# End of the attention: scaling passes for the projection's first weights and outputs on GpSimd, later splits behind the last turned keys

## The chip, the cores and the metric

One Trainium2 chip, one core. The metric is the device time of one execution in microseconds. Of the kernel before there are three timed runs: 2403.33, 2406.47 and 2407.38 us, median 2406.47. One more execution was profiled; every row of a profile here comes from it.

## What is computed

One inference step of a two-layer hybrid decoder in float32, for a prompt of 2048 tokens and 8 short samples of 4 tokens. Layer 0 runs a gated linear attention (4 heads) and a forgetting attention (4 heads of 128) side by side on one input projection; their gated outputs are put side by side and go through one output projection, whose result is added to the input. Layer 1 is a gated linear attention with its own projections. The place of this change is the end of the forgetting attention and the beginning of the output projection:

```python
logits = einsum('bthd,bshd->bhts', q, k) * scale + c_t - c_s      # causal, c = cumulative log forget values
p = softmax(logits);  o_b = einsum('bhts,bshd->bthd', p, v)
out = concatenate([o_a * silu(g_a), o_b * silu(g_b)]) @ w_out     # 1024 x 1024
x = x + out                                                        # then the next layer's RMSNorm
```

## The kernel before

A scheduler orders the instructions of each engine when the program is built; on the chip every engine takes its own queue strictly in that order, and waits where a value isn't there yet. SP's queue issues nearly all loads.

**Numbers as two halves.** TensorE multiplies float16. Every operand is split into `hi`, its float16 rounding, and `lo`, the float16 of what is left, and each product is three matmuls: hi·hi, hi·lo, lo·hi (`mm3`, lines 467 to 469). So weights and activations are scaled by a power of two and split before use. There are two ways to split a block of 128 x 512 values. In the short way ScalarE writes `hi` with the scale in it (L345 for weights, L1596 for outputs) and VectorE computes `lo` (L346, L1597). In the long way ScalarE first scales the raw block in place (L348, L1592), then writes `hi` from it unscaled (L349, L1593), and GpSimd subtracts to `lo` (L350, L1594). A weight unit of 1024 x 256 is four blocks, two of each way (`half_unit`); a piece of 256 tokens of the attention's outputs likewise (`y_pieces`, where `YPOOL` picks the blocks of the long way).

**The attention's end.** `fox_prompt` goes through 4 heads and 4 groups of 512 queries. For each block of 128 queries it computes scores `s`, adds the bias and takes the maximum on VectorE (L1200), the exponentials on ScalarE (L1208), sum and reciprocal on VectorE (L1211, L1212), and scales the rows on GpSimd (L1216). The rows `L` are then transposed on TensorE (L1236) into PSUM tiles `pt`. Such a transposed block is called a turned key here: ScalarE copies it to `th` (L1243), VectorE computes `tl` (L1244), and TensorE multiplies it with the values into `fo`. `fy` is `fo` times the gate (L1259) and goes to the outputs `yT` in memory by GpSimd's queue (L1261). The last group runs in two halves, the first with seven turned keys and the second with eight. Four buffers each hold `th` and `tl`.

**The output projection.** Four units of 256 columns (`out_units`). Unit 0 uses the raw buffer tag `yr` of two buffers, which the pieces of outputs use too: unit 0's raw weights and the first piece (`yr_19100`) take them first, the second piece (`yr_19222`) gets the weights' buffer, the third (`yr_19439`) the first piece's, and so on; the fifth piece (`yr_19463`) is the 32 sample tokens. `prepare`, mixed into the attention, splits unit 0's weights (`w_o_19102`) and the first two pieces. Behind the attention stand the other pieces, the loads of the nine row tiles of the input (L1826) and `dense(0, 3)`, which runs units 0 to 2 on TensorE and splits the next units' weights (`wr_o_19434` is unit 1's raw tile, `wr_o_19544` unit 2's, `wr_o_19613` unit 3's). The order in which the scheduler placed these among the attention's last instructions is not bound to anything but their data. A unit runs over four pairs of token tiles, then over the 32 sample rows (`few_rows`); each pair takes one of three PSUM buffers until VectorE has added it to its row tiles (L1642). SP's queue holds, in this order: unit 0's weights, pieces one and two, unit 1's weights, piece three, units 2 and 3, piece four, the next layer's first weights (`wr_Cv`), row tile 0, the sample piece, the other row tiles.

## Time and profile before

| | |
|---|---|
| median of three runs | 2406.47 us |
| the profiled execution | 2408.25 us |
| its span, first to last instruction | 2405.8 us |
| granted TensorE clock, mean of the span | 0.987 |
| busy: TensorE, VectorE, ScalarE, GpSimd | 2296.7, 1418.9, 1111.1, 744.1 us |
| first turned key of the last group's second half, on ScalarE | 1305.00 us |
| first matmul of the output projection | 1318.83 us |

Times inside the execution are microseconds from the start of the span. In a profile's row, PE is TensorE, PEld its weight loads, DVE VectorE, ACT ScalarE, POOL GpSimd, SPq the issuing queue of SP; `out<-in` names the tiles without buffer numbers, and L is the line of the kernel. A timeline row is start, duration, engine, line, operation, tiles, shape, count and, in brackets, the idle time ahead of it with what ended it. Rows of DMA issues end with the time to landing. A busy share is an average; what the change is worth is read from the stretch between about 1284 and 1345 us.

### The profile page before, as it was taken

To read this page: it belongs to the slowest core of one execution; us is meant where nothing else is said; L and a number is where in the kernel's file an instruction comes from. 1 tells how busy PE (TensorE), PEld (TensorE's weight loads), DVE (VectorE), ACT (ScalarE), POOL (GpSimd) and SP (SyncE) were. 2 spreads that over 40 slices of the span, in tenths; PEclk is the share of its full clock that TensorE was granted. 3 is DMA by queue.
4 is the path that set the end of the run, shared out by engine and by line. 5 is a ranking of instruction groups with operands and counts; after the bars stand their busy time and mean duration, and the time that the engine had idled before them with its cause. 6 is when DMAs were issued, how large, how long until landed. Compare 5 with 4: busy or idle time off the path is not lost. (4 is left out here: it accounts for less than half of the span.)

```text
span 2405.8 us, 58659 instructions
## 1 busy us (share of the span) xinstructions
PE 2296.7 (95%) x23324; PEld 1635.3 (68%) x23324; DVE 1418.9 (59%) x3345; ACT 1111.1 (46%) x2466; POOL 744.1 (31%) x839
## 2 busy tenths in 40 slices
PE   7999999999999999999997999999999999999998
PEld 5667668854655876655445876777678766666887
DVE  7556556546764548567667363665675644557554
ACT  6434243342433127466668254535443645545333
POOL 2233223112212225144465111432452222322222
PEclk9999999999999999999999999999999999999999
DMA  6231235435431276776865532122146312114453
GB/s 181 78 87 58 85 121 160 144 108 149 144 116 59 82 223 220 259 246 208 265 195 181 163 108 59 45 76 89 50 147 194 114 37 73 43 58 159 152 190 148
DMA packets 297013, 317.25 MB, mean 132 GB/s; under 512 B 39729, under 2 KB 241010, under 8 KB 296738
## 3 DMA queue, kind: packets, MB, share of 16 engines
q1 hardware_dynamic: 295234, 308.98, 40.7%
q8 instruction: 183, 3.00, 0.5%
q0 software_dynamic: 1504, 4.52, 0.5%
q14 instruction: 92, 0.75, 0.1%
HBM read 242.31 MB, written 71.11 MB: 130 GB/s over the span
## 5 line engine op out<-in xcount | busy, mean ns | idle before, releaser
L469 PE MATMUL pt_o<-w_o,act 128*128 128x256 f16 x1024 | 281.2, 275 | 4.1 <-DVE act L1597 3.9
L467 PE MATMUL pt_o<-w_o,act 128*128 128x256 f16 x1024 | 281.5, 275 | 2.4 <-ACT sg1C L523 2.4
L468 PE MATMUL pt_o<-w_o,act 128*128 128x256 f16 x1024 | 281.2, 275 | 0.0
L467 PEld LDWEIGHTS <-act 128*128 128x128 f16 x2304 | 226.9, 98 | 37.0 <-ACT act L462 4.7
L469 PEld LDWEIGHTS <-act 128*128 128x128 f16 x2304 | 226.8, 98 | 35.2 <-DVE act L1597 5.1
L468 PEld LDWEIGHTS <-act 128*128 128x128 f16 x2304 | 227.0, 99 | 33.6 <-issue 3.7
L467 PE MATMUL pt_Cv<-w_Cv,act 128*128 128x256 f16 (+1 forms) x512 | 140.3, 275 | 1.7 <-ACT act L462 0.9
L468 PE MATMUL pt_Cv<-w_Cv,act 128*128 128x256 f16 (+1 forms) x512 | 140.0, 274 | 0.0
L469 PE MATMUL pt_Cv<-w_Cv,act 128*128 128x256 f16 (+1 forms) x512 | 139.7, 274 | 0.0
L633 POOL TENSOR_TENSOR kA<-kA,fA 128x512 f32<-128x512 f32 (+1 forms) x56 | 79.0, 1411 | 191.6 <-PE gl_A L599 141.3
L1208 ACT ACTIVATE L<-L,nm,kc 128x512 f32<-128x512 f32 (+3 forms) x160 | 118.2, 740 | 37.9 <-DVE nm L1206 33.7
L633 POOL TENSOR_TENSOR kC<-kC,fC 128x512 f32<-128x512 f32 (+1 forms) x56 | 82.0, 1465 | 151.9 <-PE gl_C L599 112.5
L1216 POOL TENSOR_SCALAR L<-L,nm 128x512 f32<-128x512 f32 (+3 forms) x160 | 98.5, 629 | 65.3 <-DVE nm L1212 24.1
L1243 ACT ACTIVATE th<-pt 128x512 f16<-128x512 f32 (+3 forms) x159 | 80.6, 526 | 61.0 <-PE pt L1236 60.2
L1244 DVE TENSOR_TENSOR tl<-pt,th 128x512 f16<-128x512 f32 (+3 forms) x159 | 94.8, 609 | 22.1 <-ACT th L1243 21.0
L1236 PE MATMUL pt<-ident,L 128*128 128x128 f32 x544 | 91.9, 280 | 6.3 <-POOL L L1216 3.2
L1236 PEld LDWEIGHTS pt<-ident,L 128*128 128x128 f32 x544 | 67.2, 144 | 35.7 <-DVE tl L1244 8.7
L1360 PEld LDWEIGHTS pkt<-ident,pgcache_fox_k 128*128 128x128 f32 x512 | 57.5, 141 | 42.6 <-issue 25.1
L1360 PE MATMUL pkt<-ident,pgcache_fox_k 128*128 128x128 f32 x512 | 74.7, 278 | 7.3 <-DVE kts L1364 5.2
L467 PE MATMUL pt_Av<-w_Ai,act 128*128 128x256 f16 x256 | 70.5, 276 | 2.5 <-ACT act L462 2.5
L467 PE MATMUL fo<-th,h_v 128*128 128x512 f16 (+3 forms) x174 | 59.4, 341 | 12.4 <-ACT th L1243 9.5
L468 PE MATMUL pt_Av<-w_Ai,act 128*128 128x256 f16 x256 | 70.4, 275 | 0.8 <-POOL w_Ai L350 0.8
(950 smaller groups left out, 6756.6 us busy)
## 6 DMA issues: line engine op xcount, KB each, us to landing
pgcache_fox_k<-in_cache_fox_k SPq DMA_DIRECT2D x128, 256.0 KB, 4.3
pgcache_fox_v<-in_cache_fox_v SPq DMA_DIRECT2D x128, 256.0 KB, 3.9
yr<-yT SPq DMA_DIRECT2D x16, 1024.0 KB, 6.1
nx<-in_x_prompt SPq DMA_DIRECT2D x16, 512.0 KB, 4.9
wr_Aqf<-in_w_in_even SPq DMA_DIRECT2D x64, 128.0 KB, 3.8
wr_o<-in_w_out_even SPq DMA_DIRECT2D x32, 256.0 KB, 4.5
wr_Cv<-in_w_in_odd SPq DMA_DIRECT2D x32, 256.0 KB, 3.9
wr_Cqk<-in_w_in_odd SPq DMA_DIRECT2D x64, 128.0 KB, 3.0
```

The lines of the kernel that those rows point to most:

```text
L467: nc.tensor.matmul(ps, lh[0], rh[0], start=first, stop=False)
L468: nc.tensor.matmul(ps, lh[0], rh[1], start=False, stop=False)
L469: return nc.tensor.matmul(ps, lh[1], rh[0], start=False, stop=last)
L633: nc.gpsimd.tensor_tensor(kv[:, :, 0], kv[:, :, 0], t1.to_broadcast([P, nb, w]), ALU.mult)
L1208: self.last_exp = nc.scalar.activation(lt[:, :w], lt[:, :w], AF.Exp, bias=nm[:, 0:1], scale=ib, accum_out=nm[:, 2 + j : 3 + j])
L1216: nc.gpsimd.tensor_scalar(lt[:, :w], lt[:, :w], nm[:, 1:2], 2.0**14, ALU.mult, ALU.mult)
L1236: nc.tensor.transpose(pt[:, w : w + P], rows[b][s // 4][0][:, (s % 4) * P : (s % 4 + 1) * P], self.ident)
L1243: nc.scalar.activation(th[:, a:w], pt[:, a:w], AF.Copy),
L1244: nc.vector.tensor_tensor(tl[:, a:w], pt[:, a:w], th[:, a:w], ALU.subtract)))
L1360: nc.tensor.transpose(pk[:, j * P : (j + 1) * P], pgs[j][:, h * P : (h + 1) * P], self.ident)
```

## The change

Four edits. Unit 0's weights get `lean=True`: their two in-place scaling passes run on GpSimd. So do the four in-place scaling passes of the first two output pieces. The splits of the pieces three to five are placed, on ScalarE, behind the copy of the last turned key (`issue_after` binds ScalarE's instructions of the block behind that one in ScalarE's queue). And all ScalarE instructions of `dense(0, 3)`, so the splits of units 1 to 3, are placed behind the last `hi` of the pieces.

```diff
-    def half_unit(self, pool, pps, w, cols, key, nm, undo=None, k=1.0, also=(), raw=("wr", WU)):
+    def half_unit(self, pool, pps, w, cols, key, nm, undo=None, k=1.0, also=(), raw=("wr", WU), lean=False):
...
-                nc.scalar.activation(r, r, AF.Copy, scale=s)
+                if lean:
+                    nc.gpsimd.tensor_scalar(r, r, s, None, ALU.mult)
+                else:
+                    nc.scalar.activation(r, r, AF.Copy, scale=s)
                 nc.scalar.activation(hi, r, AF.Copy)
                 nc.gpsimd.tensor_tensor(lo, r, hi, ALU.subtract)
...
                 if layer == 0 and k in YPOOL:
-                    nc.scalar.activation(r2, r2, AF.Copy, scale=sy)
-                    nc.scalar.activation(h2, r2, AF.Copy)
+                    if (hf, c0) == (0, 0) and s < 512:
+                        nc.gpsimd.tensor_scalar(r2, r2, sy, None, ALU.mult)
+                    else:
+                        nc.scalar.activation(r2, r2, AF.Copy, scale=sy)
+                    self.last_y = nc.scalar.activation(h2, r2, AF.Copy)
                     nc.gpsimd.tensor_tensor(l2, r2, h2, ALU.subtract)
                 else:
-                    nc.scalar.activation(h2, r2, AF.Copy, scale=sy)
+                    self.last_y = nc.scalar.activation(h2, r2, AF.Copy, scale=sy)
                     nc.vector.scalar_tensor_tensor(l2, r2, sy, h2, ALU.mult, ALU.subtract)
...
-                                   raw=("yr", 256) if (hf, layer, u) == (0, 0, 0) else ("wr", WU)),
+                                   raw=("yr", 256) if (hf, layer, u) == (0, 0, 0) else ("wr", WU),
+                                   lean=(hf, layer, u) == (0, 0, 0)),
...
             units[1][0][0]()
-            for steps in pieces[2:]:
-                for step in steps:
-                    step()
+
+            with tc.issue_after(self.turns[-1][0].ins):
+                for steps in pieces[2:]:
+                    for step in steps:
+                        step()
             x1 += row_tiles(0, True)
-            drain(dense(0, 3))
+            with tc.issue_after(self.last_y.ins):
+                drain(dense(0, 3))
             drain(start(0, lambda c0, n: x1[c0 // P]))
```

The kernel after has higher line numbers: by 3 behind the weights' split (L1243 becomes L1246), by 6 behind the pieces' (L1596 becomes L1602), by 7 at the row loads. In the weights' split GpSimd's new scaling pass is L349, and ScalarE's L351, the unscaled copy L352 and GpSimd's `lo` L353; in the pieces' split they are L1596, L1598, L1599 and L1600.

ScalarE's queue before, from the third key of the last half on: `th` are keys, `wr_o_19434` and `wr_o_19544` raw weights of units 1 and 2, `w_o_19549` and `w_o_19669` their halves, `yr_19439` the third piece.

```order
L1243 ACTIVATE th_19301<-pt_19296 128x512
L1243 ACTIVATE th_19316<-pt_19311 128x512
L348 ACTIVATE wr_o_19434<-wr_o_19434,kc 128x2x256
L345 ACTIVATE w_o_19549<-wr_o_19434,kc 128x2x256
L349 ACTIVATE w_o_19549<-wr_o_19434 128x2x256
L348 ACTIVATE wr_o_19544<-wr_o_19544,kc 128x2x256
L1243 ACTIVATE th_19333<-pt_19328 128x512
L1243 ACTIVATE th_19351<-pt_19346 128x512
L349 ACTIVATE w_o_19549<-wr_o_19434 128x2x256
L1596 ACTIVATE act<-yr_19439,kc 128x2x256
L1592 ACTIVATE yr_19439<-yr_19439,kc 128x512
```

The same queue now, from the first key of that half on:

```order
L1246 ACTIVATE th_19283<-pt_19278 128x512
L1246 ACTIVATE th_19292<-pt_19287 128x512
L1246 ACTIVATE th_19301<-pt_19296 128x512
L1246 ACTIVATE th_19316<-pt_19311 128x512
L1602 ACTIVATE act<-yr_19222,kc 128x2x256 x2
L1246 ACTIVATE th_19333<-pt_19328 128x512
L1246 ACTIVATE th_19351<-pt_19346 128x512
L1246 ACTIVATE th_19368<-pt_19363 128x512
L1246 ACTIVATE th_19382<-pt_19378 128x384
L1599 ACTIVATE act<-yr_19222 128x2x256 x2
L1602 ACTIVATE act<-yr_19439,kc 128x2x256
L1598 ACTIVATE yr_19439<-yr_19439,kc 128x512
```

Only the second piece's two scaled passes are left among the eight keys; its unscaled copies, the third piece and units 1 and 2 stand behind the last one. Ahead of this place the first weights' and pieces' four scaling passes are gone too, and the second piece's two scaled passes stood ahead of the first key of the half.

GpSimd's queue before, from the store of the last but one `fy` on (`L` rows of the last two blocks, `yr_19100` the first piece, `w_o_19102` unit 0):

```order
L1261 DMA yT_76<-fy_19155 128x512
L1216 TENSOR_SCALAR L_18974<-L_18974,nm_18999 128x512
L1216 TENSOR_SCALAR L_18980<-L_18980,nm_18999 128x512
L1216 TENSOR_SCALAR L_18986<-L_18986,nm_18999 128x512
L1216 TENSOR_SCALAR L_18996<-L_18996,nm_18999 128x384
L350 TENSOR_TENSOR w_o_19102<-wr_o_19095,w_o_19102 128x2x256 x2
L1216 TENSOR_SCALAR L_19051<-L_19051,nm_19128 128x512
```

And now:

```order
L349 TENSOR_SCALAR wr_o_19095<-wr_o_19095,kc 128x512 x2
L1264 DMA yT_76<-fy_19155 128x512
L1219 TENSOR_SCALAR L_18974<-L_18974,nm_18999 128x512
L1219 TENSOR_SCALAR L_18980<-L_18980,nm_18999 128x512
L1219 TENSOR_SCALAR L_18986<-L_18986,nm_18999 128x512
L1219 TENSOR_SCALAR L_18996<-L_18996,nm_18999 128x384
L1596 TENSOR_SCALAR yr_19100<-yr_19100,kc 128x512 x2
L353 TENSOR_TENSOR w_o_19102<-wr_o_19095,w_o_19102 128x2x256 x2
L1219 TENSOR_SCALAR L_19051<-L_19051,nm_19128 128x512
```

The weights' two new passes stand ahead of the store, the first piece's two ahead of unit 0's `lo` passes and of the last block's rows. The second piece's two follow the next store, ahead of that piece's `lo`.

VectorE's queue before, from the last key of the first half on:

```order
L1244 TENSOR_TENSOR tl_19249<-pt_19244,th_19248 128x384
L1597 SCALAR_TENSOR_TENSOR act<-yr_19222,kc,act 128x2x256 x2
L1259 SCALAR_TENSOR_TENSOR fy_19275<-fo_19158,kc,fsg_18299 128x256
L1244 TENSOR_TENSOR tl_19284<-pt_19278,th_19283 128x512
L1244 TENSOR_TENSOR tl_19293<-pt_19287,th_19292 128x512
L346 SCALAR_TENSOR_TENSOR w_o_19549<-wr_o_19434,kc,w_o_19549 128x2x256
L1244 TENSOR_TENSOR tl_19302<-pt_19296,th_19301 128x512
```

And now:

```order
L1247 TENSOR_TENSOR tl_19249<-pt_19244,th_19248 128x384
L1247 TENSOR_TENSOR tl_19284<-pt_19278,th_19283 128x512
L1262 SCALAR_TENSOR_TENSOR fy_19275<-fo_19158,kc,fsg_18299 128x256
L1247 TENSOR_TENSOR tl_19293<-pt_19287,th_19292 128x512
L1247 TENSOR_TENSOR tl_19302<-pt_19296,th_19301 128x512
L1247 TENSOR_TENSOR tl_19317<-pt_19311,th_19316 128x512
L1603 SCALAR_TENSOR_TENSOR act<-yr_19222,kc,act 128x2x256 x2
L1247 TENSOR_TENSOR tl_19334<-pt_19328,th_19333 128x512
L1247 TENSOR_TENSOR tl_19352<-pt_19346,th_19351 128x512
L1247 TENSOR_TENSOR tl_19369<-pt_19363,th_19368 128x512
L1247 TENSOR_TENSOR tl_19383<-pt_19378,th_19382 128x384
```

The second piece's two `lo` passes moved from ahead of the store value `fy` to ahead of the last four keys, and no weights stand between the keys. On SP's queue the sample piece's load now follows the fourth piece at once, then come the nine row loads, and `wr_Cv` stands behind them.

## The prediction

> **What bounds the kernel now.** I read the page first (span), then the busy time in three stretches around the change, then who is waited for in the middle one.
>
> ```profile
> span 2405.8 us, 58659 instructions
> 1287.00:1319.00 32.00, 18.67 (x136) 0.94 0.71 230
> 1319.00:1427.00 108.00, 105.94 (x1008) 0.99 0.50 161
> PE fo L467 <- ACT th L1243: 6.9, 4, 2.6
> PE fo L468 <- DVE tl L1244: 3.3, 6, 1.0
> PE fo L467 <- DVE fy L1259: 2.6, 1, 2.6
> ACT act L1596 <- DMA yr<-yT: 1.9, 1, 1.9
> ```
>
> The two windows give their length, TensorE's busy time, its granted clock, DMA share and GB/s; the four rows after them give total, times and longest of a wait between 1287 and 1319 (ScalarE's from 1284). At the end of the attention TensorE works 18.7 of 32 us; as soon as the output projection runs it works 106 of 108. So a microsecond taken from the first stretch is kept, and one taken behind it has to come from little. In the first stretch TensorE waits for the turned keys `th` (ScalarE) and `tl` (VectorE), while ScalarE itself waits 1.9 us in all. What fills ScalarE there, by line (count, busy time, mean ns, idle before), and its timeline at five points:
>
> ```profile
> L1208 ACT ACTIVATE L<-L,nm,kc 128x512 f32<-128x512 f32 (+1 forms) x8 | 6.3, 795 | 0.0
> L1596 ACT ACTIVATE act<-yr,kc 128x512 f16<-128x512 f32 x6 | 4.3, 722 | 1.9 <-DMA yr<-yT 1.9
> L1592 ACT ACTIVATE yr<-yr,kc 128x512 f32<-128x512 f32 x6 | 4.3, 720 | 0.0
> L348 ACT ACTIVATE wr_o<-wr_o,kc 128x512 f32<-128x512 f32 x6 | 4.3, 719 | 0.0
> L345 ACT ACTIVATE w_o<-wr_o,kc 128x512 f16<-128x512 f32 x5 | 3.6, 719 | 0.0
> L349 ACT ACTIVATE w_o<-wr_o 128x512 f16<-128x512 f32 x5 | 3.2, 630 | 0.0
> L1593 ACT ACTIVATE act<-yr 128x512 f16<-128x512 f32 x4 | 2.5, 628 | 0.0
> 1284.05 0.71 ACT L348 ACTIVATE wr_o<-wr_o,kc 128x512 f32<-128x512 f32 x1
> 1305.00 1.06 ACT L1243 ACTIVATE th<-pt 128x512 f16<-128x512 f32 x2
> 1312.49 0.64 ACT L349 ACTIVATE w_o<-wr_o 128x512 f16<-128x512 f32 x1
> 1313.01 0.72 ACT L1596 ACTIVATE act<-yr,kc 128x512 f16<-128x512 f32 x1
> 1313.62 0.72 ACT L1592 ACTIVATE yr<-yr,kc 128x512 f32<-128x512 f32 x1
> 1317.07 0.49 ACT L1243 ACTIVATE th<-pt 128x384 f16<-128x384 f32 x1
> ```
>
> Instructions overlap, so I count from start to start: 0.61 us for a scaling pass (1313.01 to 1313.62), 0.52 for an unscaled copy (1312.49 to 1313.01), about 0.48 for a turned key (two take 1.06). Thirty-two passes for weights and outputs (all rows but L1208's exponentials) stand among the keys in the 33.5 us from 1284.05 to the end of the last key at 1317.56, the last of them just behind it.
>
> **The change, part by part.**
>
> *ScalarE.* Six scaling passes go to GpSimd (two of L348, four of L1592): 6 × 0.61 = 3.7 us. Behind the last key go three L348, two L1592, three L345, two L1596 (10 × 0.61 = 6.1) and three L349, two L1593 (5 × 0.52 = 2.6). The sixth L348 is the pass that already stood behind the last key. Together 12.4 us. ScalarE then needs 33.5 − 12.4 − 1.9 of waiting = 19.2 us, so the last key could end at 1303.3: 14.2 us earlier is the ceiling. What keeps it from that is who becomes late next.
>
> *GpSimd.* Its rows, with the idle time ahead:
>
> ```profile
> 1288.03 0.58 POOL L1261 DMA_DIRECT2D yT<-fy  x1 [4.38 <-DVE fy L1259]
> 1289.05 3.01 POOL L1216 TENSOR_SCALAR L<-L,nm 128x512 f32<-128x512 f32 x4 [0.43 <-ACT w_o L349]
> 1295.96 1.15 POOL L350 TENSOR_TENSOR w_o<-wr_o,w_o 128x512 f16<-128x512 f32 x1 [2.34 <-ACT w_o L349]
> 1298.86 2.70 POOL L1216 TENSOR_SCALAR L<-L,nm 128x512 f32<-128x512 f32 x4 [1.75 <-DVE nm L1212]
> 1301.52 2.27 POOL L1594 TENSOR_TENSOR act<-yr,act 128x512 f16<-128x512 f32 x2
> ```
>
> L1216 is the new pass's kind (one input, a column as factor, 128x512): 0.68 to 0.75 us each, hardly dearer than ScalarE's. The two for the weights fall into the 4.38 us idle ahead of the store at 1288.03 and cost nothing; without that hole they would cost 1.4. The two for the first piece stand ahead of the weights' `lo` passes and the last block's L1216, both of which end lines I need: 1.4 us on GpSimd's path. Against that the first L1216 row starts about 0.5 us earlier (ScalarE begins the exponentials 0.61 earlier): 1288.55 + 3.0 + 1.4 + 2 × 1.15 = 1295.3 for the end of the weights, and 1295.6 with 0.3 for VectorE's work beside it, against 1297.11 before. The Trainium skill's page "GPSIMD Engine Reference", section "Performance versus the Vector engine" and its table of engine selection, calls GpSimd the wrong engine for elementwise work, about twice VectorE's time with two inputs, though near line rate with one. If the factor of two held for these passes, the two on the path would take some 1.4 us more and the gain would be so much smaller; the L1216 rows speak for the one-input case, and I keep to them.
>
> ScalarE, with what is left, has done the last block's exponentials at about 1295.8: from 1284.05 eight exponentials (6.3), four keys (1.9), four passes of the first weights (2 × 0.61 + 2 × 0.52) and two of the first piece (1.2). VectorE's two small steps behind them take it to 1296.0, four passes of 2.7 us to 1298.7, where the row shows 1301.56: 2.9 us won. Before, the second half's first key nevertheless came only at 1305.00, because the second piece's passes stood ahead of it. Now it follows the transposes at once, 1299.1. That is 5.9 us. From there ScalarE has eight keys and two passes: 8 × 0.48 + 2 × 0.61 = 5.1, with 0.5 for two handoffs 1304.7, against 1317.56.
>
> *The second piece's load.* It needs the buffer that the first weights leave.
>
> ```profile
> 1297.14 0.37 SPq L1586 DMA_DIRECT2D yr<-yT  x1
> yr<-yT SPq DMA_DIRECT2D x1, 1024.0 KB, 5.4
> yr<-yT SPq DMA_DIRECT2D x1, 1024.0 KB, 8.6
> yr<-yT SPq DMA_DIRECT2D x1, 128.0 KB, 2.7
> row<-in_x_sample SPq DMA_DIRECT2D x1, 128.0 KB, 10.8
> ```
>
> The first row is its issue, the next its time to landing; the third is that of the fourth piece, the fourth and fifth are two small loads. Issued at 1295.7 it lands at 1301.1; ScalarE comes to it at about 1301.5 (four keys from 1299.1, with handoffs). Cover 0.4 us: it costs nothing, but a landing of 8.6 would cost 2.8.
>
> *VectorE's end.* The store `fy` no longer stands behind the second piece's two `lo` passes, so TensorE's 2.6 us for it go. But those two now stand ahead of four last keys.
>
> ```profile
> 1303.30 1.05 DVE L1597 SCALAR_TENSOR_TENSOR act<-yr,kc,act 128x512 f16<-128x512 f32 x1 [2.05 <-ACT act L1596]
> 1304.52 0.75 DVE L1597 SCALAR_TENSOR_TENSOR act<-yr,kc,act 128x512 f16<-128x512 f32 x1 [0.18 <-ACT act L1596]
> 1305.61 1.29 DVE L1244 TENSOR_TENSOR tl<-pt,th 128x512 f16<-128x512 f32 x2
> ```
>
> L1597 takes 0.75 alone and 1.05 beside GpSimd, and GpSimd now works on the same piece, so I take 1.05: from 1302.1, when ScalarE has done the first of the two passes, 2 × 1.05 and four keys of 0.64 make 1306.8, and TensorE's last products 0.6 to 0.8 more. The projection then starts at 1307.5 (1306.3 with 0.75 each). Its first matmul and the clock around it before:
>
> ```profile
> 1316.10 0.27 PE L467 MATMUL fo<-th,h_v 128*128 128x256 f16 x1 [1.84 <-ACT th L1243]
> 1318.83 0.42 PE L467 MATMUL pt_o<-w_o,act 128*128 128x256 f16 x1
> 1297.80:1301.20 3.40, 1.86 (x16) 1.00 0.82 247
> 1314.90:1318.30 3.40, 1.34 (x8) 1.00 1.11 342
> 1318.30:1321.70 3.40, 3.40 (x19) 0.50 1.00 237
> ```
>
> 1318.83 − 1307.5 = **11.3 us**.
>
> *The clock.* The projection's first 3.4 us ran at a granted clock of 0.50, behind a window in which TensorE was busy for 1.34 us; a window with 1.86 was followed by full clock. Half a clock for 3.4 us costs 1.7. Now TensorE has eight blocks of products and four of transposes in the last 6 us with gaps under 1 us, more than 1.86 in each 3.4, so I expect full clock: **+1.7**. The Trainium skill's "TensorE: Matmul & The Clock Gate", section "Why this matters for your kernels", asks for an idle gap over about 3 us before the clock falls. Here it fell behind a longest gap of 1.84, so the measurement differs and decides; by the page's rule the fall would have another cause and could come again, a rival below.
>
> *The work behind the last key.* The next output unit must be split by the time the first one ends.
>
> ```profile
> 1336.16 0.88 DVE L1642 SCALAR_TENSOR_TENSOR row<-pt_o,kc,row 128x256 f32<-128x256 f32 x2 [4.36 <-PE pt_o L469]
> 1341.40 0.88 DVE L1642 SCALAR_TENSOR_TENSOR row<-pt_o,kc,row 128x256 f32<-128x256 f32 x2 [4.36 <-PE pt_o L469]
> ```
>
> A pair of tiles takes 5.24 us, so the first unit ends at 1307.5 + 4 × 5.24 + 0.8 for the sample rows = 1329.3. The third piece is loaded once GpSimd has done the first (about 1301), the fourth about 1307, landing by 1315.6 at the worst of the two rows; the small sample piece is issued when the third is split (about 1313). ScalarE then has the fourth piece (4 × 0.61 + 2 × 0.52 = 3.5), the sample piece (1.3, an estimate from passes an eighth as wide) and twelve passes up to the unit's last `hi`, the later units' scaling among them (10 × 0.61 + 2 × 0.52 = 7.1); GpSimd ends it in 1.15: 1328.7. That is just in time, and I charge **−1.0** for it (between 0, with a landing of 5.4, and 2, with GpSimd held up as above). The next layer's weight loads move from ahead of the row loads to behind them on SP's queue, to about 1329; they are wanted three units of 22 us later and cost nothing while that holds.
>
> **Sum.** 11.3 + 1.7 − 1.0 = 12.0 us. Against the profiled execution (2408.25, span 2405.8) it is 2396.3; the three runs' median is 1.8 lower, and against it the forecast is **2394.5**.
>
> **The rivals.**
>
> *The clock falls again.* For: before, it did at this place. Against: the denser products. Gain 11.3 − 1.0 = 10.3, 2396.2. Chance 0.17.
>
> *The load or GpSimd becomes the last wait.* Landing of 8.6 for 5.4 costs 2.8, GpSimd's passes at twice their rows 1.4: gain 7.8, 2398.7. For: the cover is 0.4 us only. Against: the same five weight loads run beside it as before. Chance 0.17.
>
> *The next unit's weights come late.* If the sample piece's small load takes 10.8 instead of 2.7, it lands at 1323.8 and everything behind it moves: copies 2.4, the twelve passes 7.1, GpSimd 1.15, weights at 1334.5; TensorE stands 5 us; gain 7 to 8, 2399. Chance 0.10.
>
> *Slower.* On SP's queue the sample piece's load, which waits for the third piece's split, now stands ahead of all nine row loads. The projection has three PSUM buffers, so its fourth pair starts only when rows 0 and 1 are in and added, at 1307.5 + 15.7 = 1323.2. Rows issued at 1313.3 leave about 4 us. Beyond that each microsecond is lost one for one; 12 + 4 + 4.8 us of lateness make the kernel measurably slower. The third piece would have to land some 20 us after the forecast; the longest landing above is 10.8. Chance 0.04.
>
> *No change.* ScalarE's hole is real but the passes moved behind it, or something downstream, give the time back. Against: 105.94 busy of 108. Chance 0.06.
>
> **How the numbers follow.** The forecast has 0.46. About 0.2% (4.8 us) is what a measurement of this kernel can tell from no change. The forecast and the first three rivals are faster by more than that (0.90), but for some 0.03 in which two of them fall together: 0.87 faster, 0.09 within, 0.04 slower. The range reaches from the ceiling (14.2 + 1.7 less handoffs: 2391) to a late load and late weights together (gain 4.5: 2402).
>
> **What would show it.** Right: no L1592 or L348 on ScalarE between the exponentials and the last key, last `th` ending near 1305, first `pt_o` near 1307.5, granted clock 1.00 there, and at most 2 us of TensorE waiting for `w_o` at the second unit. Wrong: ScalarE waiting over 2 us for the second piece's load, VectorE's `tl` queue ending after 1309, or TensorE stopping for row tiles.

## The result, and the profile after

The changed kernel takes 2391.07 us in the median of 8 runs (2384.60 to 2401.25), the kernel before beside it 2406.83 (8 runs): a ratio of 0.9944, 95% interval 0.9930 to 0.9957. Timed once more, with 12 runs beside 35, it takes 2395.38 against 2406.94: 0.9952, 0.9936 to 0.9967. So it is faster by 0.5%, 15.8 us the first time and 11.6 the second; 12.0 had been forecast. Its runs spread wider than those of before, and the fastest had the highest granted clock (0.995), the slowest the lowest (0.986). Two executions that were slow at a low clock, one of 7425 us with two factors (below) and one of 2950 us of the kernel before, are left out of all medians and ratios.

The profiled execution took 2395.09 us. Its page gives the span; its windows are the two of before (length, TensorE's busy time, weight loads, VectorE, ScalarE, GpSimd, then granted clock, DMA share, GB/s):

```profile
span 2393.4 us, 58665 instructions
1287.00:1319.00 32.00, 27.54 (x235) 24.33 (x235) 16.70 (x33) 20.94 (x42) 23.48 (x23) 0.95 0.73 232
1319.00:1427.00 108.00, 103.67 (x991) 89.54 (x989) 59.80 (x138) 58.69 (x118) 25.73 (x25) 1.00 0.49 160
```

In the stretch between 1287 and 1319 TensorE now works 27.5 us, before 18.7; behind it 103.7 of 108, 2.3 less than before; that window holds a somewhat later part of the program now. Whom TensorE waits for between 1284 and 1345 (total, times, longest):

```profile
PE fo L470 <- ACT th L1246: 2.4, 1, 2.4
PE fo L471 <- DVE tl L1247: 1.8, 2, 1.3
PE fo L470 <- DVE mx L1203: 0.9, 1, 0.9
PE pt_o L471 <- POOL w_o L353: 0.8, 1, 0.8
```

The four waits for `th` have become one, and the wait for the store value `fy` is gone. New is the last row: the second unit's weights come 0.8 us late. ScalarE's and GpSimd's timelines, the first of ScalarE's rows being the 128x128 turned key that ends the block ahead of the stretch; it is the zero point of what follows. VectorE's last rows and TensorE's first of the projection stand at the end:

```profile
1282.68 0.28 ACT L1246 ACTIVATE th<-pt 128x128 f16<-128x128 f32 x1 [0.92 <-PE pt L1239]
1299.23 1.24 ACT L1246 ACTIVATE th<-pt 128x512 f16<-128x512 f32 x2 [2.21 <-PE pt L1239]
1301.01 1.08 ACT L1246 ACTIVATE th<-pt 128x512 f16<-128x512 f32 x2 [0.54 <-PE pt L1239]
1301.99 1.34 ACT L1602 ACTIVATE act<-yr,kc 128x512 f16<-128x512 f32 x2
1303.23 1.06 ACT L1246 ACTIVATE th<-pt 128x512 f16<-128x512 f32 x2
1304.72 0.60 ACT L1246 ACTIVATE th<-pt 128x512 f16<-128x512 f32 x1 [0.43 <-PE pt L1239]
1305.59 0.49 ACT L1246 ACTIVATE th<-pt 128x384 f16<-128x384 f32 x1 [0.28 <-PE pt L1239]
1309.90 0.72 ACT L1602 ACTIVATE act<-yr,kc 128x512 f16<-128x512 f32 x1 [2.78 <-DMA yr<-yT]
1282.45 3.11 POOL L349 TENSOR_SCALAR wr_o<-wr_o,kc 128x512 f32<-128x512 f32 x2
1290.73 3.52 POOL L1596 TENSOR_SCALAR yr<-yr,kc 128x512 f32<-128x512 f32 x2
1296.47 2.69 POOL L1219 TENSOR_SCALAR L<-L,nm 128x512 f32<-128x512 f32 x4
1302.16 3.52 POOL L1596 TENSOR_SCALAR yr<-yr,kc 128x512 f32<-128x512 f32 x2 [0.23 <-DMA yr<-yT]
1302.84 1.40 DVE L1603 SCALAR_TENSOR_TENSOR act<-yr,kc,act 128x512 f16<-128x512 f32 x2
1304.17 2.51 DVE L1247 TENSOR_TENSOR tl<-pt,th 128x512 f16<-128x512 f32 x4
1307.85 0.27 PE L470 MATMUL pt_o<-w_o,act 128*128 128x256 f16 x1
```

The zero point in the kernel before:

```profile
1283.87 0.28 ACT L1243 ACTIVATE th<-pt 128x128 f16<-128x128 f32 x1 [0.92 <-PE pt L1236]
```

ScalarE waits for TensorE's transposes among the keys now, no longer the other way round, and is done at 1306. The projection begins at 1307.85, 11.0 us earlier than before; but 1.2 us of that was won ahead of the stretch, where nothing changed, and is no merit of the change: in the fourteen traces below that key lies anywhere between 1280.64 and 1285.66. So from here on times are counted from that 128x128 key, called the last score's turned key in the expectations: 35.0 us to the projection's first product before, 25.2 now. The surprise is in GpSimd's rows. A scaling pass for weights takes 1.55 us there and one for a piece 1.76, while the softmax's row pass, the row on which the prediction priced them, still takes 0.67.

### The profile page after: what moved, and what is told of

Its sections match the earlier page's. It is cut to its first block, busy times and chain, and to the rows that moved or that the text cites. A ratio compares the mean times of both kernels' runs of the same rounds, so it can differ in the third digit from the quotient of the medians.

```text
span 2393.4 us, 58665 instructions
## 1 busy us (share of the span) xinstructions
PE 2294.6 (96%) x23324; PEld 1635.2 (68%) x23324; DVE 1414.6 (59%) x3345; ACT 1108.6 (46%) x2460; POOL 756.9 (32%) x845
## 5 line engine op out<-in xcount | busy, mean ns | idle before, releaser
L1219 POOL TENSOR_SCALAR L<-L,nm 128x512 f32<-128x512 f32 (+3 forms) x160 | 98.8, 631 | 63.3 <-DVE nm L1215 22.5
L1246 ACT ACTIVATE th<-pt 128x512 f16<-128x512 f32 (+3 forms) x159 | 80.7, 527 | 64.8 <-PE pt L1239 64.0
L472 PE MATMUL pt_Bk<-w_Bk,act 128*128 128x256 f16 x256 | 70.6, 276 | 0.0
```

The lines of the kernel that those rows point to most:

```text
L472: return nc.tensor.matmul(ps, lh[1], rh[0], start=False, stop=last)
L1219: nc.gpsimd.tensor_scalar(lt[:, :w], lt[:, :w], nm[:, 1:2], 2.0**14, ALU.mult, ALU.mult)
L1246: nc.scalar.activation(th[:, a:w], pt[:, a:w], AF.Copy),
```

## The experiments

Fourteen traces were read with two measures in us, both from the last score's turned key: to the projection's first product, and to the last product of the sample rows, which ends the projection (first and last start of those products, from the tile's row in each trace). The waits are those of the projection itself, but for 0.9 to 1.7 us for the next layer's normalised rows, which all have: `w_o` are a unit's split weights, `act` the split pieces, the sample rows are the split sample piece (`sam_o`). Medians are those of the kernel's own runs; the kernel before, beside them, had medians of 2404.5 to 2406.9. The ratios on record are not quotients of these medians and can differ from them: for the passes only, the medians lie 4.9 us apart where the ratio says 8.7.

| kernel | first product | end of projection | what TensorE waited for in the projection | median, us | ratio to before, 95% |
|---|---|---|---|---|---|
| before, two traces | 35.0, 35.3 | 130.9, 131.2 | | | |
| changed, two traces | 25.2, 24.5 | 120.5, 121.1 | `w_o` 0.8, 1.5 | 2391.1, 2395.4 | 0.9944, 0.9952 |
| passes only | 26.8 | 125.3 | sample rows 1.9 | 2399.65 | 0.9964 (0.9950 to 0.9979) |
| gates only | 29.2 | 123.5 | | 2397.32 | 0.9962 (0.9947 to 0.9977) |
| two factors | 25.6 | 120.3 | | 2392.64 | 0.9949 (0.9931 to 0.9967) |
| passes left out | 26.0 | 120.4 | | 2395.87 | 0.9950 (0.9930 to 0.9970) |
| short way | 26.9 | 121.6 | | 2394.84 | 0.9952 (0.9936 to 0.9968) |
| piece behind | 23.6 | 121.0 | `w_o` 1.2, row tile 0.8 | 2395.88 | 0.9956 (0.9940 to 0.9971) |
| two factors, piece behind | 23.4 | 122.8 | row tile 2.7 | 2395.25 | 0.9945 (0.9927 to 0.9964) |
| the same, units 1 to 3 behind the key | 23.4 | 125.5 | sample rows 3.1, `act` 1.3 | 2396.77 | 0.9961 (0.9948 to 0.9975) |
| changed, units 1 to 3 behind the key | 24.7 | 126.8 | sample rows 4.8, row tile 0.4 | 2398.23 | 0.9972 (0.9958 to 0.9985) |
| two factors, piece behind, only the next two units behind the key | 23.4 | 123.8 | sample rows 2.6, `act` 1.4 | 2394.86 | 0.9952 (0.9936 to 0.9969) |

The theory (Q) was that ScalarE's queue had bound the stretch, and that GpSimd's passes and then TensorE are what is left of it. Against it stood that the gates did it all (G) or that the gain hangs on where TensorE's clock falls (C). A gate is one of the two places of `issue_after`, a cold stretch a time at which the granted clock is about 0.5.

A long wait in the projection costs more than its length. In the five kernels in which TensorE stood 1.9 us or more at one place there, a cold stretch follows the wait, of 6.8 us in the first kernel with units 1 to 3 behind the key and of 3.4 in the others. TensorE is then busy for 95.3 to 96.9 us of the projection, and for 93.6 to 94.3 in the other six kernels with the change or a part of it.

### The two halves of the change

**Passes only**: both gates undone.

```diff
-            with tc.issue_after(self.turns[-1][0].ins):
-                for steps in pieces[2:]:
+            for steps in pieces[2:]:
...
-            with tc.issue_after(self.last_y.ins):
-                drain(dense(0, 3))
+            drain(dense(0, 3))
```

> Only the six passes go to GpSimd; both gates are undone. Of what stood behind the last turned key in the changed kernel, unit 1's first five passes (about 3.0 us of ScalarE) come back among the last four keys. Theory Q (ScalarE's queue was the bound, and GpSimd's passes and then TensorE are what is left of it): the last th ends 2 to 3 us later than in the changed kernel, TensorE was busy without a gap there, so the first product of the projection comes 1 to 3 us later, and the gain is 12 to 14.5 us of the changed kernel's 15.7 in the medians less nothing else. Rival G (the gates did it: keys ahead of the later splits; the passes on GpSimd are beside the point): the gain is under 5 us. Rival C (most of the gain is the clock: a cold stretch at the projection's start that is gone): the gain goes with the cold stretches of the profile and not with the last th; still full clock at the projection's start means over 13 us.

The last key starts 25.0 us behind the zero point against 22.9, and the first product comes 1.6 us later: as Q has it. The gain was smaller than Q's 12 to 14.5 us (0.9964 is 8.7 us), for a reason that Q had left out. The timeline of ScalarE has unit 1's passes back among the last keys, and TensorE's waits show a new one behind the key:

```profile
1305.07 0.58 ACT L1246 ACTIVATE th<-pt 128x512 f16<-128x512 f32 x1
1305.55 0.72 ACT L345 ACTIVATE w_o<-wr_o,kc 128x512 f16<-128x512 f32 x1
1306.16 0.48 ACT L1246 ACTIVATE th<-pt 128x384 f16<-128x384 f32 x1
...
PE pS_o L514 <- DVE sam_o L509: 1.9, 1, 1.9
```

Without the second gate the next layer's `wr_Cv` loads and six row loads go ahead of the sample piece on SP's queue, and the first unit's sample rows come late; TensorE's clock then fell for 3.4 us as well. **The first gate alone does nothing.** With the first gate alone, every engine's queue is the one of this kernel; with the second alone, it is the one of the changed kernel. So neither has a time of its own.

**Gates only**: no scaling pass on GpSimd.

```diff
-                    if (hf, c0) == (0, 0) and s < 512:
+                    if False:
...
-                                   lean=(hf, layer, u) == (0, 0, 0)),
+                                   lean=False),
```

> Both gates, no pass on GpSimd: the six scaling passes are ScalarE's again. Theory Q: two of the weights' and two of the first piece's cost ScalarE 4 x 0.61 = 2.4 us ahead of the last block's exponentials, and the second piece's four passes with their load stand ahead of the second half's first key again, which then comes at about 1302 to 1304 (1299.2 in the changed kernel); against that GpSimd is free of about 10 us (two of 1.55 and four of 1.76). First product of the projection at 1309.5 to 1312, gain 8 to 13 us. Rival G: nothing is lost, 14 to 16 us. Rival C: the gain goes with the cold stretches; half a clock at the projection's start again costs 1.7.

First product at 29.2 (1311.49): inside Q's span, and so is the gain (0.9962 is 9.1 us). ScalarE's timeline shows why, the second piece's passes with their load ahead of the second half's first key:

```profile
1301.07 0.72 ACT L1602 ACTIVATE act<-yr,kc 128x512 f16<-128x512 f32 x1 [1.99 <-DMA yr<-yT]
1302.92 0.71 ACT L1598 ACTIVATE yr<-yr,kc 128x512 f32<-128x512 f32 x1
1303.54 1.06 ACT L1246 ACTIVATE th<-pt 128x512 f16<-128x512 f32 x2
```

Of the 10.3 us by which the first product moved (means of two traces each), the passes alone bring 8.4 and the gates alone 5.9: they take partly the same time away. G falls, by which the gates alone would have lost nothing (14 to 16 us). The times of the two halves cannot be told from each other.

### What GpSimd's passes cost

**Two factors**: the same six passes in the form of the row pass.

```diff
-                    nc.gpsimd.tensor_scalar(r, r, s, None, ALU.mult)
+                    nc.gpsimd.tensor_scalar(r, r, s, 1.0, ALU.mult, ALU.mult)
...
-                        nc.gpsimd.tensor_scalar(r2, r2, sy, None, ALU.mult)
+                        nc.gpsimd.tensor_scalar(r2, r2, sy, 1.0, ALU.mult, ALU.mult)
```

> The changed kernel with GpSimd's six passes written with two factors (the column and 1.0), the form of the softmax's row pass, which takes 0.67 to 0.82 us in the trace where the passes with one factor take 1.55 and 1.76. Theory Q: a pass falls to 0.7 to 0.8, GpSimd is free about 1.4 to 2 us earlier for the last block's row pass, and the first product of the projection comes 1 to 2 us earlier: 1 to 2.5 us faster than the changed kernel, a few tenths of which may go to a shifted order. Rival S (the passes are dear because they come beside VectorE's and ScalarE's work on the same memory, not by their form): 1.5 to 1.8 us each again, no gain over the changed kernel within 1 us. Rival P (TensorE, busy without a gap from 1301.6, is the bound by now): passes at 0.75, but under 0.5 us gained.

```profile
1283.69 1.36 POOL L349 TENSOR_SCALAR wr_o<-wr_o,kc 128x512 f32<-128x512 f32 x2
1293.10 2.23 POOL L1596 TENSOR_SCALAR yr<-yr,kc 128x512 f32<-128x512 f32 x2
1296.47 2.70 POOL L1219 TENSOR_SCALAR L<-L,nm 128x512 f32<-128x512 f32 x4
1298.79 1.09 ACT L1246 ACTIVATE th<-pt 128x512 f16<-128x512 f32 x2 [0.53 <-PE pt L1239]
1301.87 1.33 ACT L1602 ACTIVATE act<-yr,kc 128x512 f16<-128x512 f32 x2 [1.99 <-DMA yr<-yT]
```

The weights' passes fall from 1.55 to 0.68 us, so there it is the form that makes them slow, and S falls; the pieces' fall from 1.76 to 1.1, and why these stay above 0.68 is not shown. The row pass starts 12.6 us behind the zero point (13.8 in both traces of the changed kernel), the first key 14.9 (16.6 and 15.5). But the first product is not earlier, 25.6, since the scheduler, seeing other costs, put the second piece's two copies behind two keys instead of four, where they wait 2.0 us for the load.

**Passes left out**: the six passes are dropped, so two blocks of unit 0's weights and four of the first pieces stay unscaled, and the output is another.

```diff
-                if lean:
-                    nc.gpsimd.tensor_scalar(r, r, s, None, ALU.mult)
-                else:
+                if not lean:
...
-                    if (hf, c0) == (0, 0) and s < 512:
-                        nc.gpsimd.tensor_scalar(r2, r2, sy, None, ALU.mult)
-                    else:
+                    if not ((hf, c0) == (0, 0) and s < 512):
```

> The changed kernel with the six GpSimd passes left out altogether: the first unit's two blocks of weights and four blocks of the first two pieces stay unscaled, so the output is another. What the passes still cost where they are now. Theory Q: the last block's row pass on GpSimd starts when VectorE has the reciprocals (about 1.4 us earlier), the second piece's copies no longer wait for GpSimd; first product of the projection 1 to 2 us earlier, 1 to 3 us faster than the changed kernel. Rival P (TensorE is the bound): under 0.5 us. If it is over 4 us, GpSimd's passes cost more than the row pass they hold up.

26.0 and 120.4: nothing gained, neither Q's 1 to 3 us nor a clean answer, because here too the scheduler reordered: the second piece's four copies, with 1.1 us of waiting for the load, stand ahead of the first key. What it does show is that the projection ends at 120.5 and 121.1 us with GpSimd's passes at 1.76, at 120.3 with 1.1 and at 120.4 with none.

**Short way**: unit 0's weights and the first two pieces wholly in the short way, GpSimd having nothing of them.

```diff
-                if a % 2:
+                if a % 2 or lean:
...
-                if layer == 0 and k in YPOOL:
+                if layer == 0 and k in YPOOL and not ((hf, c0) == (0, 0) and s < 512):
```

> The changed kernel with nothing of the first weights and the first two pieces on GpSimd: all their blocks go the way of the others, a scaled copy on ScalarE and the rest on VectorE (6 more copies of VectorE at 0.75 to 1.05, 6 unscaled copies of ScalarE become scaled ones, 0.09 us dearer each, and the six passes and six remainders of 1.1 on GpSimd are gone: 17 us fewer there). Theory Q (what is freed on GpSimd beyond the softmax's row pass brings nothing, and VectorE, which turns tl, becomes the late one): first product of the projection 25 to 27 us behind the last score's turned key, the changed kernel's time within 2 us or up to 2 us slower. Rival G2 (GpSimd, the busiest engine from 1287 to 1307 in the changed kernel, is the bound): 22.5 to 24 us, 1 to 2.5 us faster.

26.9 and 121.6, with a cold stretch ahead of the keys that lasts 6.8 us in place of 3.4: Q's span, and no sign of GpSimd as the bound (G2, which had 22.5 to 24, falls).

### Where a further gain goes

**Piece behind**: the second piece is split behind the last key too.

```diff
-                for steps in pieces[:2]:
+                for steps in pieces[:1]:
...
-                for steps in pieces[2:]:
+                for steps in [pieces[1][1:]] + pieces[2:]:
```

> The changed kernel with the second piece's split, too, behind the last turned key (its load stays where it is). Its two scaled copies (1.24 us) and its load no longer stand among the second half's keys, and VectorE's two passes for it stand behind the last key. Theory Q (ScalarE's, VectorE's and GpSimd's queues still set the start of the projection): from the last score's turned key to the projection's first product 25.2 us in the changed kernel's trace, here 24 to 24.7, so 0.5 to 1.2 us faster. Rival P (TensorE, busy without a gap from the fourth key on, is the bound): 25.0 to 25.3, no gain. Rival L (the piece comes late for the second pair of row tiles, which starts 5.24 us behind the first product): TensorE waits 1 us or more there for act and the kernel is slower than the changed one by that much.

The first product comes at 23.6, 0.9 to 1.6 us earlier, a little more than Q had it, and against P; the end of the projection stays, 121.0, with 1.2 us of waits for `w_o` and 0.8 for row tiles. **With two factors as well** (both diffs):

> The changed kernel with GpSimd's six passes in the form with two factors and the second piece's split behind the last turned key: the order in which the cheaper passes could pay. In the run with two factors alone the second half's first key came 14.9 us behind the last score's turned key (16.6 in the changed kernel), but the second piece's copies, moved ahead by the scheduler, then waited 2.0 us for their load. Theory Q: first key at 14.9 again, no wait for the load, and TensorE needs 8.6 us from there, as in the changed kernel: first product at 23.3 to 24.0, 1.2 to 1.9 us faster than the changed kernel. Rival P (TensorE is the bound however early the first key comes): 25.0 to 25.6, nothing gained. Rival L as in the run with the piece behind: a wait of 1 us or more for act at the second pair of row tiles eats it.

The first key comes at 14.9, the first product at 23.4: 1.1 to 1.8 us earlier than in the changed kernel, but only 0.2 earlier than with the slow passes, less than the 0.7 between the changed kernel's own two traces. So with the second piece out of the way the slow passes cost next to nothing at the first product. And what was won is lost again; TensorE's wait, and VectorE's queue at that place:

```profile
PE pt_o L470 <- DVE row L1648: 2.7, 1, 2.7
...
1324.10 0.48 DVE L1648 SCALAR_TENSOR_TENSOR row<-pt_o,kc,row 128x256 f32<-128x256 f32 x1
1326.42 1.80 DVE L346 SCALAR_TENSOR_TENSOR w_o<-wr_o,kc,w_o 128x512 f16<-128x512 f32 x2 [1.84 <-ACT w_o L345]
1328.14 1.65 DVE L1648 SCALAR_TENSOR_TENSOR row<-pt_o,kc,row 128x256 f32<-128x256 f32 x4
```

Four row tiles stand behind the remainders of later weights, which wait for ScalarE, which had waited for the third and fourth piece's loads. **Units behind the key**: the splits of units 1 to 3 released earlier, at the last key, in that kernel and in the changed one.

```diff
-            with tc.issue_after(self.last_y.ins):
+            with tc.issue_after(self.turns[-1][0].ins):
                 drain(dense(0, 3))
```

> The kernel with two factors and the second piece behind the last key, and the later units' splits released at the last turned key, no longer behind the last piece. In the run before it the projection's first product came 23.4 us behind the last score's turned key (25.2 and 24.5 in the changed kernel's two traces), but then TensorE stood 2.7 us for a row tile: VectorE's remainders of unit 1's weights were queued ahead of the row tiles and waited 1.84 us for ScalarE, which had waited for the third and fourth piece's loads with unit 1's weights queued behind them. Now unit 1's weights fill ScalarE's wait for the third piece. Theory V (that queue took the gain back): no wait for a row tile over 0.5 us, the projection's last product of the sample rows 118 to 119.8 us behind the last score's key (120.5 and 121.1 in the changed kernel), 1 to 3 us faster than the changed kernel. Rival M (the sample piece's load now stands behind the row loads, and its split comes late as in the run with the passes alone): TensorE waits about 2 us for sam_o, 120 to 122, no gain. Rival R (the row loads themselves are late): TensorE still waits for a row tile.

> The changed kernel with the later units' splits released at the last turned key (the second gate at the key, not at the last piece). In the changed kernel's trace TensorE waits 0.8 us (1.5 in the second trace) for the second unit's weights, while ScalarE stands idle 2.78 and 4.78 us for the third and fourth piece's loads. Theory V: the weights fill that idle time, the wait for w_o goes, 0.5 to 1.5 us faster than the changed kernel, under what the times can tell apart; in the trace the projection's last product of the sample rows comes 119 to 120.2 us behind the last score's key (120.5, 121.1). Rival M (the sample piece comes late behind the row loads): a wait of about 2 us for sam_o and nothing gained, or up to 3 us slower.

In the first of the two the wait for a row tile is gone, so that queue was its cause, and in the second the wait for `w_o` (V, in part); but the sample rows come 3.1 and 4.8 us late and the end of the projection moves to 125.5 and 126.8: M. In both, ScalarE has a pass for the next layer's weights ahead of the sample piece's; the rows are those of the first:

```profile
1328.98 0.75 ACT L351 ACTIVATE wr_Cv<-wr_Cv,kc 128x544 f32<-128x544 f32 x1 [7.71 <-DMA wr_Cv<-in_w_in_odd]
1329.64 0.33 ACT L1602 ACTIVATE act<-yr,kc 128x64 f16<-128x64 f32 x1
```

**Only the next two units behind the key**, in the kernel with two factors and the piece behind, so that this pass stands behind the sample piece again:

```diff
-            with tc.issue_after(self.last_y.ins):
-                drain(dense(0, 3))
+            with tc.issue_after(self.turns[-1][0].ins):
+                drain(dense(0, 1))
+            with tc.issue_after(self.last_y.ins):
+                drain(dense(1, 3))
```

> The kernel with two factors and the second piece behind the last key; of the later units only the first step (the second and third unit's weights) is released at the last turned key, the rest, with the next layer's weight loads and their passes, stays behind the last piece. In the two runs before, the sample piece's passes stood on ScalarE behind a pass for the next layer's weights, which waited 7.7 and 9.6 us for its load, and TensorE waited 3.1 and 4.8 us for the sample rows. Theory V (only that pass made the sample piece late; the second unit's weights may go early): TensorE waits under 1 us for sam_o, not for row tiles, and not for w_o; the projection's last product of the sample rows 117.5 to 119.5 us behind the last score's key (120.5 and 121.1 in the changed kernel), 1 to 3 us faster than the changed kernel. Rival M (the sample piece's load is late by itself, since it stands behind nine row loads): 2 us or more of waiting for sam_o again, nothing gained.

M again, and now without a pass in between: the load itself, issued behind the nine row loads and two loads of the next layer's weights, takes 7.5 us to land. In the changed kernel it was issued at 1315.35, ahead of them, and took 3.4.

```profile
1322.71 0.37 SPq L1589 DMA_DIRECT2D yr<-yT  x1
1330.20 0.35 ACT L1602 ACTIVATE act<-yr,kc 128x64 f16<-128x64 f32 x1 [8.90 <-DMA yr<-yT]
PE pS_o L514 <- DVE sam_o L509: 2.6, 1, 2.6
```

V's sentence that only the pass made the sample piece late is wrong. In the changed kernel the second gate keeps the sample piece's load ahead of the row loads; by these runs that is the use of releasing the later units so late.

### The two kernels once more

> The changed kernel once more, beside the three others on the same chip and for a second profile. Theory Q: 25.2 us again from the last score's turned key to the projection's first product, within 0.3, full clock at the projection's start, and 10 to 16 us under the kernel before. Rival C (the gain hangs on where the cold stretches of TensorE's clock happen to fall): a cold stretch at the projection's start again, and a gain that is smaller by 1.7.

> The kernel before once more, for a second trace. If the cold stretch of TensorE's clock at the start of its projection belongs to its thin stretch ahead of it (theory Q), it is there again, within 4 us of the projection's first product, as is the one in the middle of the last block; 34.9 us, within 0.5, from the last score's turned key to the first product. If cold stretches fall where they happen to (rival C), the first product's clock is full this time.

The changed kernel's second trace has 24.5 us to the first product, 0.7 less than the first and outside Q's 0.3: in the first trace the transposes of the last block ran at half clock. Its first keys come earlier, and so ScalarE reaches the second piece before its load has landed:

```profile
1294.89 0.37 SPq L1589 DMA_DIRECT2D yr<-yT  x1
1296.57 2.24 ACT L1246 ACTIVATE th<-pt 128x512 f16<-128x512 f32 x4 [1.17 <-PE pt L1239]
1300.39 1.34 ACT L1602 ACTIVATE act<-yr,kc 128x512 f16<-128x512 f32 x2 [1.58 <-DMA yr<-yT]
```

The kernel before has the cold stretch at the start of its projection again. Windows of its second trace, with the first matmul of the projection:

```profile
1311.84:1315.25 3.41, 1.28 (x8) 0.70 (x8) 2.76 (x5) 3.41 (x8) 0.98 (x1) 1.00 1.12 339
1315.25:1318.66 3.41, 3.41 (x18) 2.51 (x18) 1.14 (x2) 3.41 (x7) 1.92 (x4) 0.50 0.98 242
1318.66:1322.08 3.42, 3.42 (x34) 3.04 (x32) 2.85 (x2) 3.42 (x6) 2.25 (x3) 1.00 0.76 198
...
1313.12 0.27 PE L467 MATMUL fo<-th,h_v 128*128 128x256 f16 x1 [1.84 <-ACT th L1243]
1315.92 0.42 PE L467 MATMUL pt_o<-w_o,act 128*128 128x256 f16 x1
```

And the changed kernel's windows, from the last block's rows to the projection:

```profile
1293.56:1296.97 3.41, 1.26 (x9) 0.85 (x9) 1.82 (x5) 3.41 (x9) 3.41 (x4) 0.99 0.00 0
1296.97:1300.38 3.41, 3.41 (x19) 2.88 (x19) 0.87 (x2) 1.16 (x3) 3.41 (x6) 0.51 0.76 228
1300.38:1303.80 3.42, 3.42 (x34) 3.22 (x33) 3.40 (x7) 2.88 (x7) 3.19 (x4) 1.00 1.09 361
1303.80:1307.21 3.41, 3.41 (x34) 3.14 (x32) 2.80 (x5) 2.61 (x6) 2.40 (x2) 1.00 1.09 363
1307.21:1310.62 3.41, 3.41 (x35) 3.06 (x34) 0.48 (x1) 0.72 (x2) 2.29 (x3) 1.00 1.09 364
```

Before, 1.28 us of work ahead and half a clock at the start; now TensorE is busy all the time and the clock is full. The other cold stretch, that of the last block, is in both, if not at the same place.

## Why the prediction was right

The mechanism was right: ScalarE's queue held TensorE up, and emptying it brought the projection forward. The sum was too large by the traces, 12.0 for 10.2 us to the projection's end, and the times hold more than the traces locate. By its steps:

- **ScalarE's queue was the bound**: right. Six passes went to GpSimd, ten and five stand behind the last key, and ScalarE then waits 3.5 us for transposes among eight keys. With the gates only and the passes only the projection ends at 123.5 and 125.3 us, with both at 120.5 and 121.1; by the traces both kinds of edit were needed.
- **GpSimd's passes at 0.68 to 0.75**: wrong in size, 1.55 and 1.76. The step that failed is "L1216 is the new pass's kind": that row carries two factors, the new pass one. The two of the first piece took 3.5 us in place of 1.4, and the row pass of the last block started 1.2 us later than with the cheaper form. The rival with passes at twice their rows therefore came true in its premise and not in its price: it put 1.4 us on the path, and the kernels with the second piece behind show 0.2 at the first product, because TensorE needed the time anyway. The prediction had cited the Trainium skill, page "GPSIMD Engine Reference", section "Performance versus the Vector engine", for about twice VectorE's time with two inputs. No run here has these passes on VectorE, so that factor stays untested; the two-factor form at 0.68 us shows that the slow passes are not slow for being on GpSimd.
- **First key of the second half at 1299.1**: that is 15.2 us behind the zero point; measured 16.6 and 15.5, the first with half clock during the transposes.
- **The second piece's load**: 5.4 us to landing forecast; in the second trace of the changed kernel issued at 1294.89 and waited for until 1300.39, 5.5 us. The cover of 0.4 was as thin as stated: no wait in the first trace, 1.58 us in the second. By the kernel with the piece behind the last key, having it among the keys costs 0.9 to 1.6 us at the first product (the 1.6 against the trace with the half clock), which the prediction put at nothing.
- **VectorE's end**: two passes of 1.05 and four keys of 0.64 forecast, 4.7 us; measured 1.40 and 2.51, 3.9. It was not the end.
- **TensorE's own work on the eight keys**: the sum has no term for it, and it is what ended last. In the first trace TensorE is busy without a gap from the first key at 1299.23 to the first product at 1307.85, 8.6 us. From the forecast first key (15.2 us) this gives 23.8, and the forecast first product lies at 23.6, reached over VectorE's queue. The two paths happened to be equally long, so this part of the sum came out near by luck.
- **The first product**: 11.3 us earlier forecast; 10.3 by the means of the traces.
- **The clock**: 1.7 us, right, in two traces of each kernel. Rival C falls for the projection's start: all eleven kernels with the change or a part of it have the full clock at the projection's first product, and the projection's end goes with the first product and the waits behind it.
- **The next unit's weights**: 1.0 us forecast, 0.8 and 1.5 waited for.
- **Slower through the sample piece ahead of the row loads**: it did not come, TensorE waited for no row tile in the changed kernel. The sample piece behind row loads, the other way round, makes TensorE wait 1.9 to 4.8 us in four kernels, with a cold stretch after it.

To the end of the projection the traces give 131.0 less 120.8, so 10.2 us. The times give 15.8 and 11.6, with intervals that reach down to 10.3 and 7.9; the first median, 2391.07, lies at the lower end of the range (2391). Behind the projection the rest of the kernel took 991.0 and 994.0 us before and 990.2 and 989.5 in the changed kernel; the other kernels scatter more widely, from 984.2 to 995.6. The clocks on record show where a part can lie: in the second timing the mean granted clock was 0.9896 over the changed kernel's 12 runs and 0.9877 over the 35 of before, 0.0019 less. The half clock at the projection's start is 0.0007 of this difference (half of 3.4 in about 2400 us). The other 0.0012 would be about 3 us of fewer cold stretches elsewhere, an estimate from these clocks; that the change brings them about is not shown, and the cause of the remaining microseconds stays open. That the second median lies so near to the forecast is partly luck.

None of the versions tried beats the changed kernel by more than the intervals of their ratios allow to tell. Of those whose first product comes between 23.6 and 26.9, all that delay neither the sample rows nor a row tile by more than 1 us end the projection between 120.3 and 121.6 us.

## What to carry to other kernels

When one engine's in-order queue makes a busier engine wait, moving work past the critical pass pays for as long as that other engine has slack, and then stops: here 10 us came at once, and 1.8 us more at the first product came to nothing, since each thing moved on had a deadline a little later (row tiles, the next weights, a small last load). Price a moved instruction by a row with its exact form, operands and number of factors included. Give the busier engine's own work a term of its own in the sum: here it, and no helper, ended the stage. And follow a small load that gates the end of a stage: behind eleven others it took 7.5 us to land, ahead of them 3.4.

## What the runs showed of the hardware

**The form of a GpSimd pass.** A multiplication of 128x512 float32 by a column took 1.55 us with one factor and 0.68 with a second factor of 1.0, at the same place of two kernels that differ in this alone. Five traces have the one-factor form there (1.55 to 1.56), four the other (0.68). For the first piece it was 1.76 and 1.1; for the second, 1.55 to 1.76 and 0.95, or 0.68 in the three kernels with two factors in which that piece is split behind the key. Why the forms differ is not shown.

**When the clock falls.** Windows of 3.41 us laid on the times at which the clock changed, in 14 traces between about 700 and 1826 us: of 4469 at full clock, 64 had TensorE busy for less than 1.45 us, and all 64 were followed by half clock; of 209 with 1.45 to 2.35 us 45 were; of 4196 with more none. At half clock, 27 windows with less than 2.8 us busy were followed by another and 108 with more than 3.1 by full clock; of two with 3.00, one by each. The Trainium skill, "TensorE: Matmul & The Clock Gate", section "Part 1: The HAM clock gate (the "warmup" mystery)", tells of such a free-running window of about 3.4 us, and the traces agree: the cold stretches between these times are 3.41 us long, or two or three times that. Its section "Why this matters for your kernels" advises against idle gaps of over about 3 us. Here that would not have been enough: the longest gap in the window ahead of the fall shown above was 1.84 us. In these traces the window's busy time decides, but for 1.45 to 2.35 us, where either came.
